# A bidirectional DeltaNet encoder on one core: two more pairs of buffers for the weights' parts, unnormalised keys, and three columns at the start of the output product

## The chip, the core and the metric

The kernel runs on one core of a Trainium2 chip. The metric is the device time of one execution in microseconds; lower is better. The kernel before was timed in three runs.

## The reference

A trunk of two layers works on 256 tokens of 2048 channels in float32. Layer 0 is a convolution module, layer 1 a bidirectional gated DeltaNet; a SwiGLU network with 5632 hidden channels stands behind each. RMS norms precede each part, and one stands at the end. The change lies in the DeltaNet:

```python
proj = h @ w_in                         # 2048 -> q | k | v | z | beta | a
qkv = silu(depthwise_conv_centred(qkv, w_conv))
q, k = l2norm(q), l2norm(k)             # 16 key heads of 128, each for 2 value heads
# each direction, chunks of 64, decays from a, weights beta:
kk = einsum("nbhcd,nbhed->nbhce", k, k)
lower = where(strict, kk * decay * beta, 0)
sol = triangular_solve(lower + eye, [v * beta, k * beta * exp(g)])
a_qk = where(tril, einsum(q, k) * decay, 0)     # q scaled by 128 ** -0.5
# a scan over chunks then gives the outputs o of either direction
o = o * rsqrt(mean(o * o) + eps) * norm_w * silu(z)
return o.reshape(S, 4096) @ w_out
```

## The kernel before, in words

Each weight matrix comes as tiles of 128 x 128. A matrix product (`products`, line 171) makes one column of 128 outputs for all 256 tokens. It loads raw weights in chunks of eight tiles (512 KB, three buffers "raw", `raw_weights`, 153), and splits four tiles at a time (a group) into a rounded high part and the rest as low part (`halves`, 160): ScalarE casts (line 167), VectorE subtracts (168). The two parts have four buffers each, "hi" and "lo" (`HI`); a caller that gives a pool of its own gets six (`XB`). Narrow products (the DeltaNet's) run three matmuls of 256 columns for each tile: high part on the activations' high part (197), high part on their low part (198), low part (199). Wide ones run one of 512 columns (193) and one of 256 (192).

`deltanet` (478) projects columns in the order written in `ORDER` (32): four columns of q and k for two key heads (`q`), four of v (`v`), single ones of the gate z (`z`), 96 in all, each of four groups. After each group `step` advances `now` and lets generators go on that are due; a `yield n` waits for n groups. They run beside the projections at a higher priority:

- `dn_norm` (655) sums the squares of q and k, turns the sums so that tokens lie on partitions, takes the power -1/2 into `rt` (672, 673), turns that back, stores it to DRAM, loads the keys' norms spread over all partitions (`rb`) and multiplies the keys (685). Then `dn_front` (698) makes the Gram products kk and kq (709), empties them (712), applies the decays (733 to 737) and stores the matrices `am`. `dn_fill` (741) copies blocks into the workspace S.
- After every second group of heads `dn_lanes` (750) inverts 32 x 32 blocks on VectorE in S, T, w0, w1, pd and F, and `dn_inverse` (819) joins them to larger blocks with matmuls.
- `dn_heads` (879) applies inverses and scans, normalises, turns, multiplies by the gate (`zr`, read back from DRAM, 946) and stores the result to `y_d` (948). `dn_turn` (954) turns the values v beforehand.

Behind the last column the remaining steps are run off, and the output product begins: each head's y is loaded (521), split (`ys`, 229 and 230) and used by all columns of `wout`. The first two columns (526) are made side by side, tile by tile, the others one after another.

The SBUF is full in the DeltaNet stage. Tiles named in `EARLY` lie in the pool `d0`, the others in `d1`; their tags, sizes and buffers stand in `DN` (534). The tiles ys lie where d0 was: the first `OUT0` in a pool `o0`, the rest in `o1`. The order of the instructions on each engine is made by a planner that simulates the program: where several could go, the one with the higher priority does. Loads and stores go through SyncE's queue in one order.

Of the kernel before, what the change touches and what calls it, by code (L numbers as in the profile page):

```python
# [7 lines left out]
F32 = mybir.dt.float32  # L8
F32R = mybir.dt.float32r
AF = mybir.ActivationFunctionType  # L10
ALU = mybir.AluOpType
# [16 lines left out]
HP = 550  # L28
OUT0 = 17
LAST = 2500  # L30
# [14 lines left out]
HI = 4  # L45
XB = 6


# [30 lines left out]
class Trunk:  # L79
    def __init__(self, ctx, tc, x, par, cst, pw1, pw2, win, wout, gu, dn, out):  # L80
# [13 lines left out]
        self.ahead = self.more = None  # L94
        self.turn = False
        self.cst = self.cp.tile([P, NCST], F32, name="cst_sb")
        self.par = self.cp.tile([P, NRES], F32, name="par_sb")
# [62 lines left out]
    def halves(self, raw, i, n, pool=None):  # L160

        nc = self.nc
        r = raw[:, i * P : (i + n) * P]
        hi, lo = ((pool or self.wp).tile([P, CS * P], F32R, tag=t, bufs=XB if pool else HI, name=self.nm(t))[:, : n * P]
                  for t in ("hi", "lo"))
# [312 lines left out]
    def deltanet(self, next_norm):  # L478
# [3 lines left out]
        self.c_d = dram.tile([NVH, 2 * S], F32, name="c_d")  # L482
        self.rn_d = [dram.tile([4, S], F32, name=f"rn_d{g}") for g in range(NKH // 2)]
        self.a_d = [dram.tile([P, 1024], F32, name=f"a_d{v}") for v in range(NVH)]
# [4 lines left out]
        with (tc.tile_pool(name="dn0", bufs=1, reuse_waits="tile") as d0,  # L489
              tc.tile_pool(name="dn1", bufs=1, reuse_waits="tile") as d1):  # L490
            self.d0, self.d1 = d0, d1
            self.dn_setup()
# [16 lines left out]
            while self.tasks:  # L509
                self.step()  # L510
            self.tasks = None

# [3 lines left out]
        with (tc.tile_pool(name="out0", bufs=1, reuse_waits="tile") as o0,  # L516
# [8 lines left out]
            self.norm_begin()  # L525
            first = self.products(self.wout[:2], NVH, ys, wide=True, tags=("lin", "lin"))
            for j in range(KD):
                for acc in first[j] if j < 2 else self.linear(self.wout[j], NVH, ys, wide=True):
                    nc.vector.tensor_tensor(self.h[j], acc, self.h[j], op=ALU.add)
                self.norm_tile(j, *next_norm)  # L530
# [3 lines left out]
    DN = {  # L534
        "t": (S, 2), "u": (S, 2), "th": (S, 2), "s2": (S, 3), "qk": (S, 4), "sq": (S, 2), "rb": (2 * S, 1), "kk": (4 * P, 1), "kq": (4 * P, 1),
        "cb": (2 * S, 2), "e": (768, 2), "am": (1024, 2), "ar": (1024, 2), "zr": (S, 1), "xd": (16 * P, 2),
        "w0": (1024, 1), "w1": (1024, 1), "pd": (1024, 2), "F": (256, 2), "pb": (16 * P, 2), "z32": (8 * P, 1), "z64": (8 * P, 1), "bl": (8 * 64, 1),
        "w1s": (S, 2), "w2s": (S, 2), "rx": (S, 2), "ot": (S, 4), "on": (S, 2), "v": (S, 6),
        "stk": (1024, 1), "tri": (1024, 1), "na": (1, 1), "nwh": (1, 1), "dg": (128, 1), "cr": (64, 1),
        "os": (8, 2), "rn": (P, 1), "rt": (8, 4), "rs": (S, 1),  # L540
    }

    EARLY = {"stk", "tri", "z32", "z64", "bl", "xd", "w0", "w1", "pd", "F", "cb", "e", "am", "kk", "kq", "rb", "qk", "rn", "rs", "sq"}

# [9 lines left out]
    def dn_setup(self):  # L554
        nc = self.nc
        self.S, self.T = self.d("stk"), self.d("tri")
        self.z32, self.z64, self.bl, self.pb = self.d("z32"), self.d("z64"), self.d("bl"), [self.d("pb"), self.d("pb")]
        for t in (self.z32, self.z64, self.bl, *self.pb):
            nc.gpsimd.memset(t, 0.0)
        nc.gpsimd.memset(self.S, 0.0)  # L560
        nc.gpsimd.memset(self.T, 0.0)
        nc.gpsimd.memset(fv(self.T, 0, (33, 32)), 1.0)
        self.na, self.nwh = self.d("na"), self.d("nwh")
        nc.scalar.activation(self.na, self.p("alog"), AF.Exp)
        nc.vector.tensor_scalar(self.na, self.na, -1.0, None, op0=ALU.mult)
        nc.vector.tensor_scalar(self.nwh, self.p("nw"), 0.5, None, op0=ALU.mult)

# [87 lines left out]
    def dn_norm(self, g, act, sqs, xd):  # L655
# [12 lines left out]
        for b in range(2):  # L668
            nc.tensor.transpose(tp[:, 4 * b : 4 * b + 4], rs[:, b * P : (b + 1) * P], self.mat("ident")[:4, :4])
        rt = self.d("rt")  # L670
        self.rt[g] = rt
        nc.vector.tensor_scalar(rt, tp[:, :8], 4e-6, None, op0=ALU.add)
        nc.gpsimd.tensor_tensor(rt, rt, self.c("mhalf").broadcast_to([P, 8]), op=ALU.pow)
        yield STEP
        nc.tensor.transpose(tp[:8, P:], rt, self.mat("ident"))
        rn = self.d("rn", 8)
        nc.scalar.copy(rn, tp[:8, P:])
        for b in range(2):
            nc.sync.dma_start(self.rn_d[g][:, b * P : (b + 1) * P], rn[4 * b : 4 * b + 4])
        rb = self.d("rb")  # L680
        keys = self.rn_d[g].rearrange("(h r) s -> r h s", r=2)[1]
        nc.sync.dma_start(rb.rearrange("p (r s) -> p r s", r=2), keys.partition_broadcast(P))
        for r in range(2):
            k = act[2 * r + 1]
            nc.vector.tensor_tensor(k, k, rb[:, r * S : (r + 1) * S], op=ALU.mult)
        yield LAG
        yield from self.dn_front(g, act, xd)
# [10 lines left out]
    def dn_front(self, g, qk, xds):  # L698
# [3 lines left out]
        for h in range(2):  # L702
            q, k = qk[2 * h], qk[2 * h + 1]
            grams = []
            for x, tag in ((k, "kk"), (q, "kq")):
# [5 lines left out]
                gs = self.d(tag)  # L711
                nc.scalar.activation(gs, ga, AF.Copy, scale=1.0 if x is k else P ** -0.5)
                grams.append(gs)
# [27 lines left out]
    def dn_fill(self, x, xd):  # L741

        for q in range(4):
            pr = slice(32 * q, 32 * q + 32)
# [5 lines left out]
    def dn_lanes(self, inv):  # L750
# [11 lines left out]

        L, tm = self.d("w0"), self.d("w1")
        V.transpose(nt(L), tr(S))
# [6 lines left out]
        at = lambda r, c: c * 32 + r  # L771
        R = self.d("w1")

# [15 lines left out]
        for s in (4, 8, 16):  # L789
# [25 lines left out]
        V.transpose(tr(tb), nt(tm))  # L815
        V.transpose(tr(tt), tr(tm))
        inv += [tt, tb]

# [60 lines left out]
    def dn_heads(self, g):  # L879
# [46 lines left out]

        osv, rq = fv(os, 0, (4, 2), (2, 2), (1, 2)), fv(rt, 0, (2, 2), (0, 2), (4, 2))
        nc.vector.tensor_tensor(osv, osv, rq, op=ALU.mult)
        nc.vector.tensor_tensor(osv, osv, rq, op=ALU.mult)
        nc.vector.tensor_scalar(os, os, 1.0 / P, self.c("eps6"), op0=ALU.mult, op1=ALU.add)  # L930
        nc.gpsimd.tensor_tensor(os, os, self.c("mhalf").broadcast_to([P, 8]), op=ALU.pow)
# [22 lines left out]
    def dn_turn(self, n, s2, at):  # L954
        nc = self.nc
        while self.now < at:
            yield 1
        tp = self.pst("g")
        for b in range(2):
            nc.tensor.transpose(tp[:, b * P : (b + 1) * P], s2[:, b * P : (b + 1) * P], self.mat("ident"))  # L960
        v = self.d("v")
        nc.scalar.activation(v, tp[:, :S], AF.Copy, scale=0.5)
        self.v[n] = v
# [109 lines left out]
```

## Time and profile before

| | us |
|---|---|
| median of three runs | 2854.71 (2853.86 to 2856.81) |
| the profiled execution | 2851.51 |
| its span in the trace | 2849.7 |
| TensorE busy with matmuls | 2772.4 |
| VectorE busy | 2074.2 |
| ScalarE busy | 1753.7 |
| DeltaNet stage, from and to | 1102 to 1921 |

The span goes from the first to the last instruction of the program. Matmuls are pipelined: one starts before the one ahead has ended, so a busy TensorE is not TensorE at its peak. Idle time is put down to what released the engine, and PEld is TensorE's weight load. A line such as L168 is a line of the kernel before.

### The profile page before, as it was taken

Reading aid. Unit: us, or ns where it says so; the run is one execution under the profiler, and the core shown is the slowest. Engines: PE = TensorE matmul, PEld = TensorE weight load, DVE = VectorE, ACT = ScalarE, POOL = GpSimd, SP = SyncE. Lnnn points to the kernel's source line nnn. Section 1 sums busy time; section 2 is a strip of 40 time slices with the busy share of each in tenths; the row PEclk is TensorE's granted clock in tenths of the full one; section 3 lists DMA queues with packets and bytes.
Section 4 is the critical chain, followed back from the end, with each engine's and each line's share of the span. In section 5 each row is a group of like instructions: output and inputs, shape, how many; then the busy total and the mean of one; then the engine's idle time right before and its main releaser. Section 6 shows DMA issues by size and latency. Waiting matters only on the chain.

```text
span 2849.7 us, 50209 instructions
## 1 busy us (share of the span) xinstructions
PE 2772.4 (97%) x18200; PEld 2523.5 (89%) x18200; DVE 2074.2 (73%) x3895; ACT 1753.7 (62%) x3654; POOL 367.1 (13%) x427
## 2 busy tenths in 40 slices
PE   8997999999999999999999999999999999999998
PEld 8997888888888889888999999998888888888887
DVE  7999876666666667789897989756666666665555
ACT  8877555555554445667778787765455555555443
POOL 3763310000000111000000000001110000000111
PEclk9998999999999999999999999999999999999999
DMA  5442565555566665765555655576565555556664
GB/s 185 141 143 98 196 208 191 189 189 191 187 188 195 200 198 173 230 216 176 194 191 184 214 193 198 165 247 205 190 209 190 188 189 191 188 190 185 191 190 137
DMA packets 174104, 536.05 MB, mean 188 GB/s; under 512 B 19264, under 2 KB 46208, under 8 KB 173856
## 3 DMA queue, kind: packets, MB, share of 16 engines
q1 hardware_dynamic: 172560, 531.55, 58.5%
q8 instruction: 142, 2.33, 0.3%
q10 hardware_dynamic: 1296, 1.30, 0.1%
q14 instruction: 106, 0.87, 0.1%
HBM read 503.31 MB, written 29.46 MB: 187 GB/s over the span
## 4 chain that ended last, share of the span: by engine, by line
PE 79%; DVE 8%; DMA 5%; ACT 4%; issue 2%; POOL 2%; SPq 0%; DVEq 0%; POOLq 0%; ACTq 0%
PE acc L193 39%; PE acc L192 20%; PE acc L199 5%; PE acc L197 5%; PE acc L198 5%; DVE lo L168 2%; POOL a L377 2%; PE psa L849 1%; PE psb L891 1%; ACT hi L167 1%; PE psb L914 1%; DVE r L385 1%; PE acc L195 1%; ACT m L376 1%; DMA y_d<-zr 1%
## 5 line engine op out<-in xcount | busy, mean ns | idle before, releaser
L168 DVE TENSOR_TENSOR lo<-raw,hi 128x512 fp32r<-128x512 f32 x1764 | 1257.2, 716 | 621.9 <-ACT hi L167 612.0
L167 ACT CAST hi<-raw 128x512 fp32r<-128x512 f32 x1764 | 1083.0, 619 | 851.4 <-PE acc L193 664.5
L193 PE MATMUL acc<-xs,hi 128*128 128x512 f32 x2816 | 967.3, 392 | 0.0
L192 PE MATMUL acc<-xs,lo 128*128 128x256 f32 x2640 | 744.1, 282 | 0.0
L197 PE MATMUL acc<-xs,hi 128*128 128x256 f32 x2064 | 590.1, 288 | 16.8 <-ACT hi L167 10.0
L193 PEld LDWEIGHTS acc<-xs,hi 128*128 128x128 f32 x2816 | 517.0, 188 | 99.4
L199 PE MATMUL acc<-xs,lo 128*128 128x256 f32 x2064 | 590.9, 289 | 14.2 <-DVE lo L168 13.7
L198 PE MATMUL acc<-xs,hi 128*128 128x256 f32 x2064 | 587.3, 286 | 0.4 <-DVE xs L246 0.3
L192 PEld LDWEIGHTS acc<-xs,lo 128*128 128x128 f32 x2640 | 498.4, 189 | 8.4
L193 PE MATMUL acc<-hs,hi 128*128 128x512 f32 x1408 | 486.8, 391 | 0.0
L199 PEld LDWEIGHTS acc<-xs,lo 128*128 128x128 f32 x2064 | 391.9, 191 | 27.5 <-DVE lo L168 21.4
L197 PEld LDWEIGHTS acc<-xs,hi 128*128 128x128 f32 x2064 | 394.0, 191 | 24.0 <-ACT hi L167 14.6
L198 PEld LDWEIGHTS acc<-xs,hi 128*128 128x128 f32 x2064 | 394.7, 191 | 4.9 <-issue 3.2
L192 PE MATMUL acc<-hs,lo 128*128 128x256 f32 x1376 | 388.3, 282 | 0.0
L193 PEld LDWEIGHTS acc<-hs,hi 128*128 128x128 f32 x1408 | 262.4, 188 | 53.0
L192 PEld LDWEIGHTS acc<-hs,lo 128*128 128x128 f32 x1376 | 260.0, 189 | 1.6
L458 POOL TENSOR_TENSOR tg<-tg,rstd 128x256 f32<-128x256 f32 x88 | 65.7, 747 | 905.5 <-ACT tg L457 905.5
L193 PE MATMUL acc<-ys,hi 128*128 128x512 f32 x512 | 178.3, 396 | 2.4 <-DVE ys L230 2.4
L377 POOL TENSOR_TENSOR a<-a,m 128x256 f32<-128x256 f32 x170 | 148.7, 875 | 98.1 <-ACT m L376 86.3
L192 PE MATMUL acc<-ys,lo 128*128 128x256 f32 x496 | 139.0, 285 | 1.9 <-DVE lo L168 1.9
L256 POOL TENSOR_TENSOR sq<-h 128x256 f32<-128x256 f32 x59 | 54.7, 928 | 555.4 <-DVE h L469 382.2
L633 DVE SCALAR_TENSOR_TENSOR u<-t,par_sb,u 128x254 f32<-128x254 f32 (+1 forms) x256 | 120.1, 478 | 1.3 <-ACT u L629 0.4
(231 smaller groups left out, 2890.6 us busy)
## 6 DMA issues: line engine op xcount, KB each, us to landing
raw<-in_gu SPq DMA_DIRECT2D x352, 512.0 KB, 4.4
raw<-in_win SPq DMA_DIRECT2D x194, 512.0 KB, 4.0
raw<-in_dn SPq DMA_DIRECT2D x160, 512.0 KB, 3.6
raw<-in_pw SPq DMA_DIRECT2D x94, 512.0 KB, 3.9
raw<-in_wout SPq DMA_DIRECT2D x64, 512.0 KB, 3.6
a_d<-am SPq DMA_DIRECT2D x32, 512.0 KB, 5.7
ar<-a_d SPq DMA_DIRECT2D x32, 512.0 KB, 3.3
raw<-in_dn SPq DMA_DIRECT2D x32, 256.0 KB, 3.6
```

The source lines that it names most:

```text
L167: nc.scalar.copy(hi, r)
L168: nc.vector.tensor_tensor(lo, r, hi.bitcast(F32), op=ALU.subtract)
L192: nc.tensor.matmul(acc[:, S:], lo, a[:, :S], start=False, stop=False)
L193: nc.tensor.matmul(acc, hi, a, start=first, stop=last)
L195: nc.tensor.matmul(acc[:, S:], lo, a[:, :S], start=False, stop=False)
L197: nc.tensor.matmul(acc[:, :S], hi, a[:, :S], start=first, stop=False)
L198: nc.tensor.matmul(acc[:, :S], hi, a[:, S:], start=False, stop=False)
L199: nc.tensor.matmul(acc[:, :S], lo, a[:, :S], start=False, stop=last)
L256: (nc.vector if last else nc.gpsimd).tensor_tensor(sq, h, h, op=ALU.mult)
L377: nc.gpsimd.tensor_tensor(acc, acc, m, op=ALU.add)
L458: nc.gpsimd.tensor_tensor(tg, tg, rstd, op=ALU.mult)
L633: nc.vector.scalar_tensor_tensor(u[:, lo:hi], t[:, lo + s : hi + s], w(i), u[:, lo:hi], op0=ALU.mult, op1=ALU.add)
```

## The change

Every third split in the DeltaNet stage takes its two tiles from d1, where each has two buffers: six in all. Room for these 8 KB a partition comes from d0: rb and rn are gone, w1 is replaced by the workspace S itself, and pd and F have one buffer in place of two. As S is now written until `dn_lanes` is done, `dn_fill` waits for that. The keys are not normalised any more: their factor is applied where the Gram products are emptied, in two instructions, each with a scale from `rt`, and on the other side at the emptying of the turned values, also in two. `rt` has 24 columns: the factors squared, the factors, and half of their reciprocals. The output product begins with three columns, and 26 tiles ys lie in o0.

```diff
-OUT0 = 17
+OUT0 = 26
+MORE = 2
@@ halves
+        self.nsplit += 1
+        bufs = XB if pool else HI
+        if self.parts is not None and self.nsplit % 3 == 0:
+            pool, bufs = self.parts, MORE
-        hi, lo = (... bufs=XB if pool else HI ...)
+        hi, lo = (... bufs=bufs ...)
@@ deltanet
-            self.d0, self.d1 = d0, d1
+            self.d0, self.d1, self.parts = d0, d1, d1
...
-            self.tasks = None
+            self.tasks = self.parts = None
-            first = self.products(self.wout[:2], NVH, ys, wide=True, tags=("lin", "lin"))
+            first = self.products(self.wout[:3], NVH, ys, wide=True, tags=("lin", "lin", "lin"))
             for j in range(KD):
-                for acc in first[j] if j < 2 else self.linear(...):
+                for acc in first[j] if j < 3 else self.linear(...):
@@ DN, EARLY
-  "rb": (2 * S, 1), "w1": (1024, 1), "pd": (1024, 2), "F": (256, 2), "rn": (P, 1), "rt": (8, 4),
+  "pd": (1024, 1), "F": (256, 1), "rt": (24, 4),
@@ dn_norm
+        nc.vector.tensor_scalar(rt[:, :8], tp[:, :8], 4e-6, None, op0=ALU.add)
+        nc.gpsimd.tensor_tensor(rt[:, 8:16], rt[:, :8], self.c("mhalf").broadcast_to([P, 8]), op=ALU.pow)
+        nc.vector.scalar_tensor_tensor(rt[:, 16:24], rt[:, :8], 0.5, rt[:, 8:16], op0=ALU.mult, op1=ALU.mult)
+        nc.vector.tensor_tensor(rt[:, :8], rt[:, 8:16], rt[:, 8:16], op=ALU.mult)
         self.rt[g] = rt
-        nc.vector.tensor_scalar(rt, tp[:, :8], 4e-6, None, op0=ALU.add)
-        nc.gpsimd.tensor_tensor(rt, rt, self.c("mhalf").broadcast_to([P, 8]), op=ALU.pow)
         yield STEP
-        nc.tensor.transpose(tp[:8, P:], rt, self.mat("ident"))
-        rn = self.d("rn", 8)
-        nc.scalar.copy(rn, tp[:8, P:])
-        for b in range(2):
-            nc.sync.dma_start(self.rn_d[g][:, b * P : (b + 1) * P], rn[4 * b : 4 * b + 4])
-        rb = self.d("rb")
-        ...
-        nc.sync.dma_start(rb.rearrange("p (r s) -> p r s", r=2), keys.partition_broadcast(P))
-        for r in range(2):
-            k = act[2 * r + 1]
-            nc.vector.tensor_tensor(k, k, rb[:, r * S : (r + 1) * S], op=ALU.mult)
-        yield LAG
@@ dn_front
-                nc.scalar.activation(gs, ga, AF.Copy, scale=1.0 if x is k else P ** -0.5)
+                for a in range(2):
+                    r = slice(2 * a * P, 2 * (a + 1) * P)
+                    nc.scalar.activation(gs[:, r], ga[:, r], AF.Copy, scale=self.rt[g][...])
@@ dn_fill
+        while self.filled:
+            yield 1
+        self.filled = x == 1
@@ dn_lanes
-        L, tm = self.d("w0"), self.d("w1")
+        L, tm = self.d("w0"), S
-        R = self.d("w1")
+        R = S
-        tm = self.d("w1")
+        tm = S
...
+        self.filled = False
@@ dn_turn
-        while self.now < at:
+        while self.now < at or n // 4 not in self.rt:
             yield 1
-        nc.scalar.activation(v, tp[:, :S], AF.Copy, scale=0.5)
+        for b in range(2):
+            c = slice(b * P, (b + 1) * P)
+            i = 16 + 4 * b + n % 4 // 2 * 2 + 1
+            nc.scalar.activation(v[:, c], tp[:, c], AF.Copy, scale=rt[:, i : i + 1])
```

The factors that the keys no longer carry are also taken into account in `dn_setup` and at the end of `dn_heads` (lines 566 and 927 to 930), by other constants and other columns of `rt`.

## Rows read from the trace of the kernel before

**Rows 1.** The head of the profile's page: the span, then the busy time of each engine with its share of the span and its number of instructions.

```profile
span 2849.7 us, 50209 instructions
...
PE 2772.4 (97%) x18200; PEld 2523.5 (89%) x18200; DVE 2074.2 (73%) x3895; ACT 1753.7 (62%) x3654; POOL 367.1 (13%) x427
```

**Rows 2.** Busy time by stretch (us from the span's start: length, then busy time and number of instructions of TensorE's matmuls, its weight loads, VectorE, ScalarE and GpSimd, then granted clock, DMA share, GB/s). The first row is the DeltaNet stage, the second its end and the beginning of the output product, the third the rest of the output product.

```profile
1102.00:1921.00 819.00, 786.63 (x6437) 754.44 (x6437) 684.32 (x1489) 596.84 (x1453) 32.10 (x21) 0.99 0.61 200
1921.00:1945.00 24.00, 19.71 (x93) 16.22 (x93) 13.75 (x31) 10.77 (x25) 0.00 (x0) 0.86 0.64 206
1944.00:2101.00 157.00, 157.00 (x906) 138.93 (x905) 107.72 (x162) 78.11 (x130) 24.95 (x30) 1.00 0.61 195
```

**Rows 3.** Waits of TensorE's matmuls from 1098 to 1935 us: who waited for whom, us in total, times, the longest.

```profile
PE acc L199 <- DVE lo L168: 11.5, 17, 1.8
PE acc L197 <- DVE t L628: 3.8, 3, 1.8
PE acc L197 <- ACT hi L167: 3.3, 4, 1.4
PE acc L193 <- DVE ys L230: 2.4, 1, 2.4
PE psg L709 <- DVE qk L685: 2.4, 3, 1.0
...
PE acc L192 <- DVE lo L168: 1.9, 1, 1.9
...
PE psb L891 <- ACT hi L167: 0.9, 1, 0.9
```

**Rows 4.** TensorE's timeline at the beginning of the DeltaNet stage, undisturbed: the first and the last of 17 matmuls, each of 256 columns (start, duration, line, operation).

```profile
1100.07 0.28 PE L198 MATMUL acc<-xs,hi 128*128 128x256 f32 x1
...
1101.93 0.28 PE L199 MATMUL acc<-xs,lo 128*128 128x256 f32 x1
```

**Rows 5.** The same view at 1185.7 us, behind a wait of 1.69 us for the low part of a weight tile.

```profile
1185.74 0.39 PE L199 MATMUL acc<-xs,lo 128*128 128x256 f32 x1 [1.69 <-DVE lo L168]
1185.96 0.37 PE L197 MATMUL acc<-xs,hi 128*128 128x256 f32 x1
```

**Rows 6.** ScalarE's timeline ahead of that wait.

```profile
1182.05 3.16 ACT L747 ACTIVATE stk<-xd 32x256 f32<-32x256 f32 x8 [0.63 <-DVE xd L735]
1185.23 0.62 ACT L167 CAST hi<-raw 128x512 fp32r<-128x512 f32 x1
```

**Rows 7.** Waits of VectorE in the DeltaNet stage (1098 to 1935 us).

```profile
DVE zr L947 <- DMA zr<-z_d: 19.2, 13, 2.6
DVE qk L685 <- DMA rb<-rn_d: 12.6, 5, 3.9
...
DVE am L733 <- DMA a_d<-am: 9.7, 4, 3.4
```

**Rows 8.** Waits of ScalarE in the same stretch.

```profile
ACT hi L167 <- PE acc L198: 68.3, 109, 2.0
...
ACT hi L167 <- DMA raw<-in_win: 17.7, 12, 2.9
```

**Rows 9.** Two links of the chain of waits that ended last (start, length): the norms' way through DRAM, for group 6.

```profile
1701.35 2.94 DMA rn_d<-rn
1704.30 3.75 DMA rb<-rn_d
```

**Rows 10.** Groups of instructions on ScalarE from 1098 to 1935 us (line, operation, shapes, count | busy us, mean ns of one | idle before, and what ended it).

```profile
L167 ACT CAST hi<-raw 128x512 fp32r<-128x512 f32 x397 | 240.0, 616 | 109.9 <-PE acc L198 68.3 <-DMA raw<-in_win 17.7 <-DMA raw<-in_wout 6.7
...
L935 ACT ACTIVATE ot<-ot,os 128x128 f32<-128x128 f32 x64 | 19.6, 396 | 0.0
...
L944 ACT ACTIVATE on<-psb,nwh 128x256 f32<-128x256 f32 x32 | 14.5, 469 | 2.6 <-DVE zr L947 1.8 <-PE psb L942 0.7
...
L962 ACT ACTIVATE v<-psg 128x256 f32<-128x256 f32 x32 | 12.0, 376 | 2.6 <-PE psg L960 2.6
...
L712 ACT ACTIVATE kq<-psg 128x512 f32<-128x512 f32 x16 | 9.4, 590 | 5.3 <-PE psg L709 5.3
```

**Rows 11.** The same on VectorE.

```profile
L168 DVE TENSOR_TENSOR lo<-raw,hi 128x512 fp32r<-128x512 f32 x397 | 268.6, 685 | 38.9 <-ACT hi L167 34.8 <-issue 1.7
...
L685 DVE TENSOR_TENSOR qk<-qk,rb 128x256 f32<-128x256 f32 x16 | 6.1, 421 | 12.6 <-DMA rb<-rn_d 12.6
```

**Rows 12.** Two stretches of 40 us whose granted clock is below full (columns as in rows 2).

```profile
1178.00:1218.00 40.00, 38.12 (x298) 36.19 (x297) 28.74 (x58) 28.93 (x67) 1.64 (x1) 0.96 0.77 246
...
1738.00:1778.00 40.00, 39.48 (x329) 39.49 (x330) 38.17 (x103) 25.93 (x67) 0.00 (x0) 0.96 0.61 202
```

**Rows 13.** The end of the stage in stretches of 10 us (columns as in rows 2).

```profile
1920.00:1930.00 10.00, 6.61 (x35) 5.08 (x33) 4.15 (x7) 3.93 (x9) 0.00 (x0) 1.00 0.51 158
1930.00:1940.00 10.00, 9.11 (x36) 7.82 (x37) 5.96 (x15) 4.32 (x11) 0.00 (x0) 0.66 0.67 224
...
1950.00:1960.00 10.00, 10.00 (x59) 8.86 (x58) 7.60 (x12) 5.07 (x9) 1.73 (x2) 1.00 0.70 225
```

**Rows 14.** The loads of the heads' outputs from DRAM: their count, durations and first and last start.

```profile
L521 SPq DMA_DIRECT2D y<-y_d x32: 319/382/1582, 1864.0 to 1939.9; - x32
```

**Rows 15.** The stretch of 10 us with the highest DMA rate (last column, GB/s).

```profile
1870.00:1880.00 10.00, 9.15 (x80) 8.89 (x79) 7.84 (x18) 7.84 (x22) 0.00 (x0) 1.00 0.94 306
```

**Rows 16.** The DMA issues of the output product's weights (count, size, median us from issue to landing).

```profile
raw<-in_wout SPq DMA_DIRECT2D x64, 512.0 KB, 3.6
```

More of the change, by code (lines that the diff above doesn't have):

```diff
@@ L95, in __init__ @@
         self.turn = False
+        self.parts, self.nsplit = None, 0
         self.cst = self.cp.tile([P, NCST], F32, name="cst_sb")
@@ L163, in halves @@
         r = raw[:, i * P : (i + n) * P]
-        hi, lo = ((pool or self.wp).tile([P, CS * P], F32R, tag=t, bufs=XB if pool else HI, name=self.nm(t))[:, : n * P]
-                  for t in ("hi", "lo"))
+        self.nsplit += 1
+        bufs = XB if pool else HI
+        if self.parts is not None and self.nsplit % 3 == 0:
+            pool, bufs = self.parts, MORE
+        hi, lo = ((pool or self.wp).tile([P, CS * P], F32R, tag=t, bufs=bufs, name=self.nm(t))[:, : n * P] for t in ("hi", "lo"))
         with self.tc.high_priority(WP):
@@ L482, in deltanet @@
         self.c_d = dram.tile([NVH, 2 * S], F32, name="c_d")
-        self.rn_d = [dram.tile([4, S], F32, name=f"rn_d{g}") for g in range(NKH // 2)]
         self.a_d = [dram.tile([P, 1024], F32, name=f"a_d{v}") for v in range(NVH)]
@@ L525, in deltanet @@
             self.norm_begin()
-            first = self.products(self.wout[:2], NVH, ys, wide=True, tags=("lin", "lin"))
+            first = self.products(self.wout[:3], NVH, ys, wide=True, tags=("lin", "lin", "lin"))
             for j in range(KD):
-                for acc in first[j] if j < 2 else self.linear(self.wout[j], NVH, ys, wide=True):
+                for acc in first[j] if j < 3 else self.linear(self.wout[j], NVH, ys, wide=True):
                     nc.vector.tensor_tensor(self.h[j], acc, self.h[j], op=ALU.add)
@@ L534 @@
     DN = {
-        "t": (S, 2), "u": (S, 2), "th": (S, 2), "s2": (S, 3), "qk": (S, 4), "sq": (S, 2), "rb": (2 * S, 1), "kk": (4 * P, 1), "kq": (4 * P, 1),
+        "t": (S, 2), "u": (S, 2), "th": (S, 2), "s2": (S, 3), "qk": (S, 4), "sq": (S, 2), "kk": (4 * P, 1), "kq": (4 * P, 1),
         "cb": (2 * S, 2), "e": (768, 2), "am": (1024, 2), "ar": (1024, 2), "zr": (S, 1), "xd": (16 * P, 2),
-        "w0": (1024, 1), "w1": (1024, 1), "pd": (1024, 2), "F": (256, 2), "pb": (16 * P, 2), "z32": (8 * P, 1), "z64": (8 * P, 1), "bl": (8 * 64, 1),
+        "w0": (1024, 1), "pd": (1024, 1), "F": (256, 1), "pb": (16 * P, 2), "z32": (8 * P, 1), "z64": (8 * P, 1), "bl": (8 * 64, 1),
         "w1s": (S, 2), "w2s": (S, 2), "rx": (S, 2), "ot": (S, 4), "on": (S, 2), "v": (S, 6),
         "stk": (1024, 1), "tri": (1024, 1), "na": (1, 1), "nwh": (1, 1), "dg": (128, 1), "cr": (64, 1),
-        "os": (8, 2), "rn": (P, 1), "rt": (8, 4), "rs": (S, 1),
+        "os": (8, 2), "rt": (24, 4), "rs": (S, 1),
     }
-    EARLY = {"stk", "tri", "z32", "z64", "bl", "xd", "w0", "w1", "pd", "F", "cb", "e", "am", "kk", "kq", "rb", "qk", "rn", "rs", "sq"}
+    EARLY = {"stk", "tri", "z32", "z64", "bl", "xd", "w0", "pd", "F", "cb", "e", "am", "kk", "kq", "qk", "rs", "sq"}
     def d(self, tag, rows=P):
@@ L565, in dn_setup @@
         nc.vector.tensor_scalar(self.na, self.na, -1.0, None, op0=ALU.mult)
-        nc.vector.tensor_scalar(self.nwh, self.p("nw"), 0.5, None, op0=ALU.mult)
+        nc.vector.tensor_scalar(self.nwh, self.p("nw"), 0.5 * P ** -0.5, None, op0=ALU.mult)
     def dn_gates(self):
@@ L711, in dn_front @@
                 gs = self.d(tag)
-                nc.scalar.activation(gs, ga, AF.Copy, scale=1.0 if x is k else P ** -0.5)
+                for a in range(2):
+                    r = slice(2 * a * P, 2 * (a + 1) * P)
+                    nc.scalar.activation(gs[:, r], ga[:, r], AF.Copy, scale=self.rt[g][:, 4 * a + 2 * h + 1 : 4 * a + 2 * h + 2])
                 grams.append(gs)
@@ L816, in dn_lanes @@
         V.transpose(tr(tt), tr(tm))
+        self.filled = False
         inv += [tt, tb]
@@ L925, in dn_heads @@
         self.heads_done[g] = True
-        osv, rq = fv(os, 0, (4, 2), (2, 2), (1, 2)), fv(rt, 0, (2, 2), (0, 2), (4, 2))
+        osv, rq = fv(os, 0, (4, 2), (2, 2), (1, 2)), fv(rt, 8, (2, 2), (0, 2), (4, 2))
         nc.vector.tensor_tensor(osv, osv, rq, op=ALU.mult)
         nc.vector.tensor_tensor(osv, osv, rq, op=ALU.mult)
-        nc.vector.tensor_scalar(os, os, 1.0 / P, self.c("eps6"), op0=ALU.mult, op1=ALU.add)
+        nc.vector.tensor_scalar(os, os, P ** -2.0, self.c("eps6"), op0=ALU.mult, op1=ALU.add)
         nc.gpsimd.tensor_tensor(os, os, self.c("mhalf").broadcast_to([P, 8]), op=ALU.pow)
@@ L960, in dn_turn @@
             nc.tensor.transpose(tp[:, b * P : (b + 1) * P], s2[:, b * P : (b + 1) * P], self.mat("ident"))
-        v = self.d("v")
-        nc.scalar.activation(v, tp[:, :S], AF.Copy, scale=0.5)
+        v, rt = self.d("v"), self.rt[n // 4]
+        for b in range(2):
+            c = slice(b * P, (b + 1) * P)
+            i = 16 + 4 * b + n % 4 // 2 * 2 + 1
+            nc.scalar.activation(v[:, c], tp[:, c], AF.Copy, scale=rt[:, i : i + 1])
         self.v[n] = v
```

1 line of the change is left out of this document (removed).

## The prediction

> **What bounds the kernel now.** TensorE does: on the page it is busy for 97% of the span, VectorE for 73%, ScalarE for 62% [rows 1]. I read the page first, then busy time by stretch, since the change lies in the DeltaNet stage and in the product behind it. From 1102 to 1921 us matmuls are busy for 786.6 of 819 us, at a granted clock of 0.99, so 32.4 us are idle; the 24 us behind them have a clock of 0.86, and from 1944 us on the output product has no idle time at all [rows 2]. Everything that can be won is thus between 1100 and 1945 us. The waits of TensorE's matmuls there tell what it lacks [rows 3]: mostly the low part of a weight tile from VectorE (11.5 us in 17 waits), the high part from ScalarE (3.3 and 0.9 us), an accumulator that VectorE empties late (3.8 us), the normalised keys (2.4 us). The timeline shows one of these waits [rows 5], and ScalarE ahead of it [rows 6]: it copies blocks for 3.16 us between two casts. Undisturbed, matmuls start (1101.93 - 1100.07) / 16 = 0.116 us apart [rows 4], so a group of four weight tiles (12 matmuls) is 1.4 us of work. With four buffers, three groups lie ready: 4.2 us. An engine that is away for longer, counting the way back through ScalarE and then VectorE, leaves TensorE dry. VectorE is away often: it waits in its queue for transfers, 12.6 us for the norms' way through DRAM, 19.2 us for gates, 9.7 us for a store that still reads its buffer [rows 7]. And buffers are what the split waits for: ScalarE's casts stood 68.3 us, in 109 waits, until matmuls gave a buffer back, and 17.7 us for raw weights [rows 8].
>
> **The change part by part.** The sum is made against the profiled execution, 2851.51 us (a span of 2849.7 us and 1.8 us around it), 3.2 us below the median of 2854.71 us; I take the difference off the median. About 0.2% (5.7 us) is what a measurement of this kernel can tell from no change.
>
> *Six buffers.* Every third split of the stage goes to two further pairs of buffers. They are used in turn, so five groups can lie ready, 5 x 1.4 = 7.0 us, 2.8 us more than before. The longest wait that they are to cover is 1.8 us [rows 3]. The waits for parts sum to 15.7 us in 22 waits. A matmul lasts 0.28 us and the next starts 0.12 us behind it, so a wait loses some 0.17 us more than its idle time shows: 22 x 0.17 = 3.7 us. Together 19.4 us. All would go if each wait stood alone; several follow one another before the buffers have filled again, and where raw weights are late more buffers of parts are empty too. Between none and 19.4 us I take three quarters: -14.5 us. What is late next are the accumulators (3.8 us) and the heads' own links, which stay.
>
> *Clock.* Behind the wait at 1185.7 us matmuls start 0.22 us apart instead of 0.116 [rows 5]: the lower of the clock's two levels. The stretch of 40 us there has a clock of 0.96, and so has that from 1738 us [rows 12]: 4% of 40 us, 1.6 us each. In the whole stage 1% of 819 us, 8 us, is lost in this way [rows 2]. I count the two: -3.2 us, between 0 and -8.
>
> *Keys without norm.* Eight times the change removes a transpose, a copy, two stores, a load that spreads the norms over all partitions, and two VectorE multiplies of 0.42 us (16, 6.1 us [rows 11]) that stood 12.6 us in front of VectorE's queue [rows 7]. The matmuls of dn_front waited 2.4 us for them in three waits, 2.9 us with the hidden part: -2.9 us. The VectorE time frees low parts, and is counted above. On SP's queue 24 transfers go, and the raw weights behind them move up.
>
> *Scales at the evictions.* In place of the multiply, each Gram product (32) is emptied by two instructions of 256 columns with a scale from a tile, and each of 32 value tiles by two of 128 columns. The nearest rows [rows 10]: one of 512 columns took 590 ns, one of 256 with such a scale 469 ns, so 2 x 469 - 590 = 348 ns more, 11.1 us in all. A value tile took 376 ns, two halves at 396 ns would take 416 ns more, 13.3 us in all. ScalarE, busy for 597 of 819 us [rows 2], has room, and casts go ahead of it by priority; the one buffer "g" in PSUM is held some 0.35 us longer, 64 times. On the path between -1 us (half an eviction done sooner) and 22 us (each held in full); the next user of "g" comes two steps later, some 4 us, so I take +2 us. The added VectorE operations on 8 columns cost nothing: they are done three steps, 6 us, ahead of their use, on an engine busy for 684 of 819 us [rows 2].
>
> *One workspace in dn_lanes.* S serves as w1, and pd and F have one buffer each. All three are written and read by VectorE in one order, so nothing is awaited that wasn't. The new wait is dn_fill's: it holds until the lanes of the pair before are done. Counted in steps (one per group, 384 in the stage, so 819 / 384 = 2.1 us each): the lanes of groups 0 and 1 run from step 68 to 100, the fill of group 2 comes at 112; for group 4 it is 180 against 188, for group 6 it is 256 against 264. It never binds, and behind it stands only its own generator. dn_turn's wait for rt doesn't bind either, as the norms of a group are done tens of steps before its values.
>
> *The end.* dn_norm loses a LAG of six steps, so the last pair's lanes, inverse and heads come up to 6 x 2.1 = 13 us earlier, and the DRAM way of 2.94 + 3.75 us [rows 9] goes with it. That meets the stall at the end: where 59 matmuls run in 10 us, 35 and 36 ran from 1920 to 1940 us, at a clock of 0.66 in the second half [rows 13]: 47 too few, 47 x 10 / 59 = 8.0 us. The last heads' outputs are read back by 1939.9 us [rows 14]. Three columns instead of two give 32 x 0.347 = 11 us more work at that point (0.347 us a tile and column: 157 us / 906 x 2 [rows 2]). But here parts is None: four buffers again, three raw tiles, and three columns take three of each at once. I bound the opener's own price below (12.4 us). Between -8 and +4 us I take -3.
>
> *Removed from TensorE.* Eight transposes, 8 x 0.116 = 0.9 us. The move of tiles from o1 to o0 changes no time: the loads begin once the inverse is done, before as after.
>
> Sum: -14.5 - 3.2 - 2.9 + 2 - 3 - 1 = -22.6 us; 2854.7 - 22.6 = **2832 us**. The order on each engine comes from a planner's simulation, which I can't foresee; that is the widest part of the range.
>
> **The rivals.** *A: the cover only moves the wait* (chance 0.20). In-order VectorE still stands before zr and am for 28.9 us [rows 7], and raw weights, still in three buffers, come late as before [rows 8]; the parts go half as well, -10 us, the clock gives nothing, and the end nothing: with the keys -2.9 and the evictions +2, some -10 us: 2844 us. For it speaks that ScalarE's 17.7 us are at the raw tiles already; against it that 68.3 us are at the parts.
>
> *B: the opener starves* (0.08, the slower side). Three columns need three raw tiles of 512 KB at once, 1.57 MB, 5.1 us at the highest rate seen, 306 GB/s [rows 15] (one alone lands in 3.6 us [rows 16]), then a cast of 0.62 and a subtraction of 0.69 us [rows 10, 11]: 6.4 us, against 12 x 0.347 = 4.2 us that the group in work covers; 2.2 us at each of three changes of chunk, 6.7 us. At each of seven changes of group two of three columns are split only when TensorE gives their buffers back, some 0.8 us late, 5.7 us. Sum 12.4 us, and with the clock at half in it up to 20. This decides if the body gives less than the opener takes: with A's -10 and 20, 2865 us. Against it: TensorE stands still there today anyway.
>
> *C: more was lost than idle time shows* (0.12). Then every term of the sum pays in full: 19.4 + 8 + 2.9 + 8 + 1 = 39 us, 2815 us. Idle time of pipelined matmuls understates, as the 0.17 us above show. The Trainium skill (Perfetto Trace Analysis, Identifying the Most-Contended Engine) says that matmul busy time is a poor measure and the weight loads' share a better one. By it 819 - 754.4 = 64.6 us of the stage are open [rows 2], twice the 32.4; the trace agrees in direction, but small products and transposes are in that too.
>
> *D: nothing that can be measured* (0.05), if the planner spends the room on running further ahead at the wrong places.
>
> **How the numbers follow.** The forecast has 0.55, and its own range is 2822 to 2842 us (parts at 8 to 19 us, the end from -8 to +4). The range of 8 in 10 takes in A and part of C: 2818 to 2850. Faster by over 0.2%, below 2849: forecast 0.54, C 0.12, A 0.15, 0.81 in all. Slower, above 2860.4: B and a stray 0.01, 0.08. The rest, 0.11, is within.
>
> **What would show it.** Right: the waits of matmuls for low and high parts fall under 6 us between 1100 us and the stage's end; no wait for rb; ScalarE busy some 20 us longer; the first ys matmul some 10 us earlier, and no slice of 10 us with under 50 matmuls at the end. Wrong: as many waits for parts, now behind raw tiles (A); idle time or half clock in the first 35 us of the output product (B); matmuls that wait for kk, kq or v (the evictions were under-priced).

## The result and the profile after

The changed kernel takes **2830.63 us** (median of four runs, 2829.84 to 2833.88) against 2854.28 us for the kernel before: a ratio of **0.9923 [0.9911, 0.9936]**. That is 23.6 us less by the medians and 22 us by the ratio, which the comparisons below use. The profiled execution took 2831.13 us. The head of its page, to be read against [rows 1]:

```profile
span 2829.3 us, 50192 instructions
...
PE 2754.5 (97%) x18192; PEld 2508.4 (89%) x18192; DVE 2070.5 (73%) x3895; ACT 1760.6 (62%) x3710; POOL 367.6 (13%) x427
```

The span is 20.4 us shorter. Nearly all of it (20.1 us) lies between the stage's beginning at 1102 us and the end of the output product, at 2099.8 us before and 2079.7 us after. By stretch, columns as in [rows 2]; the first row now ends where the first matmul of the output product stands (1878.6 us, before 1913.3 us):

```profile
1102.00:1879.00 777.00, 755.67 (x6333) 729.89 (x6332) 671.24 (x1468) 590.91 (x1472) 30.71 (x20) 1.00 0.62 204
1879.00:1945.00 66.00, 53.81 (x301) 45.73 (x301) 35.38 (x71) 33.35 (x81) 5.78 (x6) 0.90 0.58 186
1944.00:2079.00 135.00, 135.00 (x779) 119.40 (x778) 90.77 (x133) 66.62 (x110) 20.73 (x24) 1.00 0.60 191
```

The first row shows a body at a granted clock of 1.00, where before there were five drops to the lower level, 17.1 us together. The second row is the other side: the output product opens 35 us earlier, but the 66 us behind its opening hold 12.2 us without work at a clock of 0.90, where the 32 us behind the opening held 4.3 us before. TensorE's waits in the body, as in [rows 3]:

```profile
PE pssum L668 <- ACT sq L656: 3.9, 3, 2.4
PE acc L202 <- DVE t L633: 3.0, 2, 1.6
...
PE acc L202 <- ACT hi L172: 2.0, 3, 1.2
PE acc L204 <- DVE lo L173: 1.8, 5, 0.9
```

The low parts, first in [rows 3] with 11.5 us in 17 waits, stand at 1.8 us in 5, and high and low parts together at 3.8 us in 8, up to the opening (2.5 us more for low parts behind it). No wait for normalised keys is left, and none names kk, kq or v. What ScalarE's casts wait for, as in [rows 8]:

```profile
ACT hi L172 <- PE acc L203: 49.2, 65, 2.6
ACT hi L172 <- DMA raw<-in_win: 43.0, 27, 4.8
```

The wait for a free buffer of parts fell by 19 us, and that for raw weights rose by 25 us: the raw tiles are what is late next. The two evictions that changed, as in [rows 10]:

```profile
L968 ACT ACTIVATE v<-psg,rt 128x128 f32<-128x128 f32 x64 | 20.1, 364 | 6.6 <-DVE rx L908 4.3 <-PE psg L963 1.9
...
L710 ACT ACTIVATE kk<-psg,rt 128x256 f32<-128x256 f32 x32 | 13.4, 469 | 2.4 <-PE psg L705 2.2
```

They cost 469 and 364 ns each, as the nearest rows had said (469 and 396), but kk, kq and v together keep ScalarE busy 16 us longer than before, and no wait of TensorE names them. The end in stretches of 10 us, as in [rows 13], and the two longest waits of TensorE between 1879 and 1945 us:

```profile
1900.00:1910.00 10.00, 9.05 (x55) 7.81 (x54) 4.71 (x9) 6.97 (x17) 1.91 (x1) 1.00 0.45 134
1910.00:1920.00 10.00, 6.59 (x37) 5.13 (x35) 3.01 (x5) 3.76 (x8) 0.00 (x0) 0.94 0.66 230
1920.00:1930.00 10.00, 3.64 (x11) 3.06 (x12) 2.62 (x7) 1.16 (x4) 0.00 (x0) 0.50 0.28 91
1930.00:1940.00 10.00, 10.00 (x53) 8.70 (x53) 9.29 (x17) 6.41 (x13) 3.87 (x5) 0.88 0.53 173
```

```profile
PE acc L198 <- DVE ys L235: 8.6, 1, 8.6
PE acc L197 <- DVE lo L173: 2.5, 4, 1.1
```

From 1920 to 1930 us only 11 matmuls run, at the lower clock: all three columns stand for 8.6 us before one head's output. Why it is late shows in SyncE's queue at the end of the stage (start, duration, operation):

```profile
1908.15 0.38 SPq L951 DMA_DIRECT2D y_d<-zr  x1
...
1913.22 0.33 SPq L949 DMA_DIRECT2D zr<-z_d  x1
...
1915.79 0.32 SPq L951 DMA_DIRECT2D y_d<-zr  x1
...
1917.96 0.32 SPq L949 DMA_DIRECT2D zr<-z_d  x1
...
1921.73 0.32 SPq L951 DMA_DIRECT2D y_d<-zr  x1
1923.41 0.32 SPq L949 DMA_DIRECT2D zr<-z_d  x1
1926.00 0.32 SPq L951 DMA_DIRECT2D y_d<-zr  x1
```

There is one buffer zr. So the last heads go one behind the other: a store to DRAM, a load of the next gate into the buffer that the store has freed, a multiply, the next store. The last store starts at 1926.0 us, 4.5 us earlier than before (1930.5 us), although TensorE was ready 35 us earlier.

### The profile page after: what moved, and what is told of

It is laid out like the page before. It is cut to its first block, busy times and chain, and to the rows that moved or that the text cites. A ratio compares the mean times of both kernels' runs of the same rounds, so it can differ in the third digit from the quotient of the medians.

```text
span 2829.3 us, 50192 instructions
## 1 busy us (share of the span) xinstructions
PE 2754.5 (97%) x18192; PEld 2508.4 (89%) x18192; DVE 2070.5 (73%) x3895; ACT 1760.6 (62%) x3710; POOL 367.6 (13%) x427
## 4 chain that ended last, share of the span: by engine, by line
PE 81%; DVE 6%; ACT 5%; DMA 5%; issue 2%; POOL 1%; SPq 0%; DVEq 0%; POOLq 0%; ACTq 0%
PE acc L198 40%; PE acc L197 20%; PE acc L204 5%; PE acc L203 5%; PE acc L202 5%; DVE lo L173 2%; POOL a L382 1%; DMA raw<-in_win 1%; ACT hi L172 1%; PE psa L852 1%; PE psb L894 1%; DMA y_d<-zr 1%; PE acc L200 1%; PE psb L917 1%; DVE r L390 1%
```

## The experiments

Ratios are to the kernel before, run beside each. The last five columns are in us, from the profiled executions. "Opening" is the first matmul of the output product; idle time of TensorE and time at the lower clock are given for the body (1102 us to the opening) and the end (from there to the last matmul of the output product; behind 1945 us only three_alone, four_buffers, six_three and four_columns have any of it); "last store" is the start of the last store of a head's output. Two profiled executions lie over 5 us above the median of their kernel: short_chain's (2840.28 against 2834.9 us) and four_columns' (2849.22 against 2843.45 us).

| kernel | ratio | opening | idle, body / end | lower clock, body / end | last store |
|---|---|---|---|---|---|
| before | 1 | 1913.3 | 32.4 / 4.3 | 17.1 / 6.8 | 1930.5 |
| the change | 0.9923 | 1878.6 | 21.3 / 12.2 | 0 / 13.7 | 1926.0 |
| six_alone | 0.9977 | 1871.9 | 17.1 / 22.5 | 10.2 / 30.7 | 1924.5 |
| keys_alone | 0.9956 | 1896.0 | 23.8 / 9.2 | 17.1 / 10.2 | 1918.5 |
| three_alone | 1.0027 | 1916.5 | 33.9 / 8.9 | 20.5 / 3.4 | 1934.8 |
| two_columns | 0.9955 | 1880.9 | 17.0 / 18.6 | 20.5 / 17.1 | 1925.9 |
| four_buffers | 0.9979 | 1901.8 | 26.9 / 7.8 | 17.1 / 0 | 1931.2 |
| six_three | 0.9982 | 1875.7 | 20.2 / 23.7 | 6.8 / 27.3 | 1931.9 |
| keys_lag | 0.996 | 1893.0 | 23.1 / 13.3 | 10.2 / 13.7 | 1919.9 |
| short_chain | 0.9948 | 1886.8 | 20.1 / 13.1 | 17.1 / 10.2 | 1934.8 |
| zr_four | 0.9913 | 1870.9 | 16.1 / 12.8 | 10.2 / 6.8 | 1919.7 |
| opener_parts | 0.9911 | 1866.2 | 14.0 / 10.4 | 6.8 / 13.7 | 1913.9 |
| all_three | 0.9921 | 1864.8 | 14.3 / 13.2 | 6.8 / 10.2 | 1913.1 |
| four_columns | 0.997 | 1915.9 | 37.8 / 0.2 | 49.4 / 5.2 | 1909.5 |

**One part at a time.** *six_alone*: the kernel before, with the fifth and sixth buffer and the shared workspaces that make room for them.

```diff
+ if self.parts is not None and self.nsplit % 3 == 0: pool, bufs = self.parts, MORE
- L, tm = self.d("w0"), self.d("w1")
+ L, tm = self.d("w0"), S
```

> The kernel before with the shared workspaces and six buffers alone: keys still normalised through DRAM, two columns at the start of the output product. My theory: waits for parts fall from 15.7 to under 6 us, the clock's drops mostly go, and the time is 12 to 20 us under the kernel before, 2834 to 2842 us; the drop of VectorE's wait for rb adds at most 4 us to that in the full change. Rival (VectorE's queue is what mattered): with rb still awaited for some 12 us the waits for parts stay over 10 us and the gain is under 6 us.

Measured 2847.61 us, 0.9977 [0.9967, 0.9986], 6.6 us less. Its two stretches:

```profile
1102.00:1872.00 770.00, 752.88 (x6299) 729.49 (x6299) 668.51 (x1452) 570.84 (x1387) 31.12 (x20) 0.99 0.63 204
1872.00:1945.00 73.00, 50.51 (x264) 42.42 (x263) 34.28 (x75) 36.83 (x97) 4.40 (x4) 0.79 0.58 180
```

Idle time in the body falls from 32.4 to 17.1 us, and the opening comes 41 us earlier. But the heads end only 6 us earlier (1924.5 us), so 22.5 of the 73 us behind the opening are idle, at a clock of 0.79. The buffers do in the body what they are for; alone, most of it is given back at the end.

*keys_alone*: the changed kernel with four buffers, two columns and the workspaces and the 17 tiles ys in o0 of before, so the unnormalised keys by themselves.

```diff
- self.d0, self.d1, self.parts = d0, d1, d1
+ self.d0, self.d1, self.parts = d0, d1, None
```

> The kernel before with unnormalised keys alone: four buffers, the old workspaces, two columns. My prediction put 2.9 us on the matmuls' wait for the normalised keys and took 2 us off for the evictions; by it 2850 to 2856 us. If the shorter way from the keys to the lanes brings the heads' end forward by the 13 us that the prediction counted, 2840 to 2847 us.

Measured 2840.4 us, 0.9956 [0.9941, 0.9971], 12.6 us less: the only one of the three that pays much alone.

```profile
1102.00:1896.00 794.00, 770.15 (x6370) 743.81 (x6369) 677.84 (x1479) 599.93 (x1493) 29.80 (x19) 0.99 0.62 202
1896.00:1945.00 49.00, 39.78 (x221) 34.31 (x220) 30.31 (x57) 25.58 (x56) 4.13 (x5) 0.90 0.61 192
```

```profile
L948 SPq DMA_DIRECT2D y_d<-zr x4: 319/322/327, 1901.4 to 1918.5; - x4
```

The body is 8.6 us less idle, and the last heads' outputs (the row gives the first and last start of the last four stores) are stored 12 us earlier than before.

*three_alone*: the kernel before, whose output product begins with three columns.

```diff
- first = self.products(self.wout[:2], NVH, ys, wide=True, tags=("lin", "lin"))
+ first = self.products(self.wout[:3], NVH, ys, wide=True, tags=("lin", "lin", "lin"))
```

> The kernel before with three columns at the start of the output product, nothing else. Theory now: the heads' chain ends near 1926 us in every version, the projections end when TensorE lets them, and the columns at the start are filler between the two. Before has 32 us between its first product of ys (1913 us) and the end of its trouble (1945 us), with 8 us lost in it; a third column covers most of that: 2844 to 2850 us. Rival: without more buffers three columns starve, and the time is 2854 us or more.

Measured 2860.44 us, 1.0027 [1.0016, 1.0039], **7.7 us more**. The wait that rival B had priced is there, from 1916 to 1960 us:

```profile
PE acc L192 <- DVE lo L168: 6.5, 8, 3.4
```

Three columns take parts faster than four buffers give them, 6.5 us in 8 waits, while TensorE had waited for heads for 2.4 us only in this place [rows 3]: there is little to fill, and something to lose.

**One part undone.** *two_columns* is the change with `self.wout[:2]`; *four_buffers* is the change with `self.parts = None` in the stage.

> The changed kernel with two columns at the start of the output product instead of three. Its trace shows a wait of 8.6 us there for the last heads' outputs. If the third column is filler that covers this wait (32 tiles, 11 us of work), two columns make the wait longer by up to 10 us: 2834 to 2842 us. Rival, the starving opener of the prediction: three columns are split too late, and two win 2 to 6 us: 2825 to 2829 us. If the planner merely puts other projections there, 2829 to 2833 us.

> The changed kernel without the two further pairs of buffers; its keys, workspaces and three columns stay. My theory: the buffers carry the gain of the stage's body. Waits of matmuls for the parts come back to 10 to 16 us between 1100 us and the opener (3.8 us with six), two to five drops to half clock come back, and the time rises from 2830.6 to 2842 to 2850 us. Rival: the gain comes from the norms' way through DRAM that is gone, and from the room that this gives VectorE; then the waits for parts stay under 8 us and the time is 2831 to 2836 us.

two_columns: 2840.17 us, 0.9955 [0.994, 0.997]; the waits for the heads' outputs at the end are two, 8.3 and 7.2 us, and the third column fills about one of them. four_buffers: 2846.83 us, 0.9979 [0.9969, 0.9988]; waits for parts in the body are back, though with 8.6 us they stay under the 10 to 16 us expected. The largest wait is another: for `pd`, the inverted blocks that VectorE makes in dn_lanes.

```profile
PE psa L852 <- DVE pd L818: 8.5, 4, 3.2
PE acc L204 <- DVE lo L173: 6.2, 13, 1.0
...
PE acc L202 <- ACT hi L172: 2.4, 4, 1.4
```

*six_three* (six_alone with three columns) completes the set.

> Six buffers and shared workspaces with three columns, keys still normalised through DRAM. Six buffers alone gave 2847.6 us: the projections end 42 us earlier, and 22 us of the 73 behind them were idle. Theory: the third column (11 us of filler) turns that into time, 2834 to 2841 us, and the keys' part is the rest to 2830.6. Rival: the unnormalised keys are what lets the chain end in time, and without them the third column wins under 3 us: 2845 to 2850 us.

Measured 2848.93 us, 0.9982 [0.9972, 0.9991]. From 1876 to 1945 us:

```profile
1876.00:1945.00 69.00, 46.17 (x244) 38.57 (x242) 27.61 (x63) 32.53 (x91) 1.63 (x1) 0.80 0.55 180
```

Without the new keys the heads end at 1931.9 us, and the third column, used up at the same late output, does not help: 22.8 us are idle here, 23.7 with what follows.

The eight settings together, as ratio x 2854 us: keys are worth -12.6 us alone, -6.2 with six buffers, -13.7 with three columns, -16.9 with both; six buffers -6.6, -0.3 with keys, -12.8 with three columns, -16.0 with both; three columns +7.7, +1.5 with six buffers, +6.6 with keys, -9.2 with both. (The workspaces go with six buffers, and in four_buffers too, where they are a rival: of the +6.6 us of the third column beside the keys, some or all can be theirs. Against keys_alone, four_buffers is no more idle at the end, 7.8 against 9.2 us, but 3.1 us more in the body, and its matmuls wait 8.5 us for `pd`, against 0.8 us. No run has the keys with the workspaces, four buffers and two columns, or the workspaces alone.) With intervals of some 3 to 4 us either way on each ratio, the differences of 10 us and more between settings stand: alone the three add to -11.5 us, together they give -22.

**The lag.** *keys_lag* is keys_alone with `yield LAG` put back ahead of `yield from self.dn_front(...)`; *short_chain* is the change with the other lag cut, `yield LAG` to `yield 1` behind dn_lanes.

> Keys alone, with the LAG of six steps put back in dn_norm that the change removes. Keys alone gave 2840.4 us, 12.8 under the kernel before, and its last heads' output came 12 us earlier (1918.5 against 1930.5 us). If the six steps carry that, the last output comes at 1926 us or later and the time goes back to 2847 to 2852 us. If VectorE's queue, free of the wait for rb, carries it, the time stays at 2838 to 2843 us.

> The changed kernel with a lag of one step instead of six between dn_lanes and dn_inverse. In its trace 15 us lie there for the last pair. Theory: the heads' chain sets the end, so the last output comes 8 to 10 us earlier than 1926 us, the wait of 8.6 us for it goes under 3 us, and the time is 2820 to 2825 us. Rival: the planner's order at the end sets it, and the time stays within 2828 to 2834 us.

keys_lag: 2840.01 us, 0.996 [0.9946, 0.9974], the same as keys_alone.

```profile
L949 SPq DMA_DIRECT2D y_d<-zr x4: 320/323/326, 1902.7 to 1919.9; - x4
```

The last store moves by 1.4 us, not by the 13 us that six steps of 2.1 us would be. short_chain: 2834.9 us, 0.9948 [0.9933, 0.9963], 4 us slower than the change by the medians and 7 by the ratios, whose intervals just touch; the last store is at 1934.8 us. The 15 us that I had expected between the last pair's lanes and its inverse are not there: in the change its first matmul waits for the lanes and starts as they end.

```profile
1788.79 2.00 PE L852 MATMUL psa<-pd,z 128*128 128x64 f32 x16 [0.59 <-DVE pd L818]
```

Work ordered by priority runs ahead of the step in which it is written, so neither of these two lags in steps was time. Whether the short lag is really slower, and why, is not settled: its waits in the body are those of the change, and the 17.1 us at the lower clock, some 8.5 us of work, belong to the profiled execution, the slowest of its four (see the last section).

**The end.** *zr_four* is the change with four buffers zr.

```diff
- "zr": (S, 1)
+ "zr": (S, 4)
```

> The changed kernel with four buffers instead of one for zr, in which a head's gate is read back, multiplied and stored. With one buffer each of the last four heads goes through store, load, multiply in turn, some 5 to 6 us each, from 1908 to 1926 us. If that row of waits sets the arrival of the last outputs, the last store comes 8 to 12 us earlier, TensorE's wait of 8.6 us and the half clock around it mostly go, and the time is 2818 to 2824 us. Rival: the heads' own chain or SyncE's queue sets it, and the time stays within 2828 to 2832 us.

Measured 2828.71 us, 0.9913 [0.9898, 0.9928]: the turn through one buffer is gone, the last store comes 6.3 us earlier, and the single wait of 8.6 us is no longer there. Only 1.9 us of it show in the time, and the intervals overlap: 12.8 us at the end are still idle, in many small waits, and the body has 10.2 us at the lower clock. The single buffer is thus a cause of that one wait; most of the time lost at the end stays without it.

*opener_parts* is zr_four with two more buffers of parts for the output product's opening, too (and 22 tiles ys in o0); *all_three* is opener_parts with the short lag.

```diff
+ self.parts, self.nsplit = o0, 0
  first = self.products(self.wout[:3], NVH, ys, wide=True, tags=("lin", "lin", "lin"))
+ self.parts = None
```

> Four zr buffers as in zr_four (2828.7 us), and two further pairs of parts for the third of the three columns at the start of the output product, so that each column has two pairs. In zr_four TensorE waits 3.7 us there for low parts and 0.9 us for high ones. If that is the price of opening with three columns on four pairs, these waits go and the time is 2822 to 2826 us. If the raw tiles, still three, are what comes late, 2827 to 2831 us.

> The short lag, four zr buffers and the opener's own parts together. If the three add, 2812 to 2820 us; if the short chain already covers the end, 2819 to 2824 us; if the planner's order undoes one by another, 2826 us or more.

opener_parts: 2824.91 us, 0.9911 [0.9896, 0.9926], the lowest median of all, but not to be told from the change. all_three: 2828.42 us, 0.9921 [0.9906, 0.9936]. The stretches of opener_parts and its last stores:

```profile
1102.00:1866.00 764.00, 750.04 (x6298) 727.74 (x6296) 665.65 (x1454) 582.97 (x1444) 29.74 (x21) 1.00 0.63 204
1866.00:1945.00 79.00, 68.61 (x384) 58.63 (x383) 46.69 (x96) 44.26 (x115) 7.79 (x8) 0.91 0.65 209
```

```profile
L953 SPq DMA_DIRECT2D y_d<-zr x4: 319/342/383, 1912.3 to 1913.9; - x4
```

The body is the best of all (14.0 us idle), the last output is stored 12 us earlier than in the change, and still 10.4 us are idle at the end, because the opening has moved up by 12 us too.

*four_columns* is zr_four with four columns, whose parts lie in the room that the stage leaves (`pool=o1`).

> The changed kernel with four zr buffers and four columns at the start of the output product, with six buffers of parts and three more raw tiles of their own for them. Theory: between the last projection (about 1871 us) and the last ys (1930 us) TensorE has 59 us to fill with the heads' matmuls and 32 x 0.347 = 11 us for each column; the fourth, and parts that are split in time, take most of the 13 us that stand idle there with three: 2817 to 2824 us. Rival: the longest wait is for the heads' own matmuls, and filler changes nothing more: 2826 to 2830 us.

Measured 2843.45 us, 0.997 [0.9958, 0.9983].

```profile
1102.00:1916.00 814.00, 776.18 (x6390) 750.60 (x6388) 680.69 (x1497) 604.43 (x1514) 31.35 (x21) 0.97 0.62 201
1916.00:1945.00 29.00, 29.00 (x154) 25.32 (x155) 15.75 (x26) 13.47 (x25) 0.00 (x0) 0.91 0.57 185
```

```profile
PE acc L198 <- ACT hi L172: 7.4, 1, 7.4
PE psb L947 <- ACT ot L940: 5.8, 1, 5.8
```

```profile
1910.96 1.33 SPq L159 DMA_DIRECT2D raw<-in_wout  x3
1915.25 1.14 ACT L172 CAST hi<-raw 128x512 fp32r<-128x512 f32 x2 [2.20 <-DMA raw<-in_wout]
```

The end up to 1945 us has no idle time (29.00 of 29.00 us), but the opening had to wait until 1916 us. The 7.4 us are a wait for a high part, whose cast waited in turn for raw weights: SyncE issues their loads only at 1910.96 us, behind the last heads' stores. Whether the queue held them back or room that the stage still filled, no run separates. The body ran 49 us at the lower clock in this execution, the slowest of six.

## Why the prediction held, and where it did not

The sum was -22.6 us; -23.6 us were measured by the medians, -22 by the ratio. The trace of the change shows the mechanism that was forecast, fewer waits for parts. That the sum came so close is luck in part: a term that was too small, one with the wrong sign and one that was not seen made up for each other. Of the signs that were to show it right, the waits for parts and the missing wait for rb came; the opening was not some 10 but 35 us earlier, the end has slices with 37 and 11 matmuls, and idle time and the lower clock behind the opening, a sign of B, are there.

- **Six buffers, -14.5 us: the waits as forecast, the price only in company.** 15.7 us of waits for parts [rows 3] became 3.8 us. Undone in the change (four_buffers), the buffers are worth 16.0 us; of the waits behind that, 4.8 us are for parts (8.6 against 3.8) and 6.4 us for `pd` (8.5 against 2.1), which the sum did not have. Alone the buffers are worth 6.6 us, beside the keys with two columns 0.3 us, which the working, term by term, did not allow for.
- **Clock, -3.2 us: open.** In the two profiles all five drops in the body went, 17.1 us at half, some 8.5 us: the bound of 8, not the two drops that I counted. But their going is not shown to be the change's doing. two_columns, with the same buffers and less idle time in the body, has 20.5 us at the lower clock. And over the whole span the profiled execution of the kernel before has a mean granted clock of 0.990, where 42 others of the same kernel have 0.990 to 0.994, 0.992 in the mean; the four of the change have 0.991 to 0.992. The term should have been a range from the start.
- **Keys, -2.9 us: mis-sized.** Alone they are worth 12.6 us, [8.3, 16.8]. I had priced the matmuls that waited for keys, and put the rest into a step that the runs refute: the six steps of LAG (keys_lag). What else pays is not separated: VectorE's queue stands 12.6 us less for the norms [rows 7], 24 transfers leave SyncE's queue, and the way through DRAM leaves each chain of heads. No run divides these three. The last group's norms are taken 12 us earlier in keys_alone (the power at 1684.2 against 1696.2 us), so this chain is already 12 us ahead where that group's own way through DRAM would begin.
- **Evictions, +2 us: not seen.** The prices held (469 and 364 ns); no matmul of the trace after waits for kk, kq or v. ScalarE is busy 6.9 us longer on the page, where 20 were forecast; but the page counts time in which two instructions overlap once, and with each instruction counted in full it is 19.8 us (1922.0 against 1902.3 us).
- **The end, -3 us: wrong sign.** From the opening to 1945 us, idle time rose from 4.3 to 12.2 us and time at the lower clock from 6.8 to 13.7 us. The step that failed is the one that brought the last pair 13 us earlier: the last pair's lanes did end 9.7 us earlier (1788.7 against 1798.4 us), but the last store came only 4.5 us earlier, behind the single buffer zr, while the faster body brought the opening 35 us earlier. The third column was then needed to fill a gap that the change itself had opened (two_columns).
- **Workspaces, 0 us: not shown.** The matmuls that wait for `pd` are the inverse's first: 2.1 us in two waits in the body of the change, 1.3 us in two before, but 8.5 us in four in four_buffers, and none in six_alone, both with the same workspaces. These never ran by themselves, so whether they or something else makes the lanes late there stays open.

**The rivals.** *A* named the right thing (raw tiles late: 17.7 to 43.0 us on ScalarE), but it did not reach TensorE, whose waits for high parts are 2.0 us in the body. *B* is true of the third column alone (three_alone, +7.7 us against 12.4 forecast); in the change the opener's waits for low parts are 2.5 us, as the columns stand before a late output anyway. *C* held in its idea: from 1102 us to the output product's end 20.1 us went, of which TensorE's idle time is only some 3 us. To see the rest, I took for each pair of successive matmuls the time from start to start, less the lower quartile of the same pair of shapes over the fourteen kernels' traces (the end reaches to the output product's last matmul):

| us lost | before | the change | keys_alone | six_alone | three_alone |
|---|---|---|---|---|---|
| body | 85.5 | 57.8 | 69.4 | 52.9 | 87.4 |
| end | 9.0 | 18.9 | 12.7 | 34.9 | 15.3 |

In the body of the change, waits over 0.3 us fell from 39.1 to 24.7 us, the lower clock from 7.9 to 0, the losses below 0.3 us each, which no view of idle time shows, from 38.5 to 33.1. So the body gained 27.7 us, 7.9 of them by the clock alone, and the end took 9.9 us back; six_alone gained 32.6 and gave back 25.9. The Trainium skill (Perfetto Trace Analysis, Identifying the Most-Contended Engine) says that the weight loads' share tells more than that of the matmuls. The trace agrees in direction again: time without weight loads fell from 90.1 to 82.9 us between the same two points (997.8 us with 907.7 us of loads, 977.7 with 894.8). That is twice what idle time shows, and still only 7.2 of 20.1 us.

## What to carry to other kernels

Before you price more buffers in the middle of a stage, follow the chain that ends the stage: if it does not get shorter, TensorE arrives earlier and waits there instead, and the gain must be carried by work that can fill that place (here a third column, which cost time as long as there was no gap). Price a part within the setting in which it will run: alone the three parts gave 11.5 us, together 22. In an order made by priorities, a lag written in steps need not be time, as two here were not: look in the trace whether the engine waits there at all. And before you price a clock from one profile, look at the granted clock of the kernel's other executions.

## What the runs showed that was not expected

The same wait can be followed by a drop of the clock or not. At 1678 us, in the change and in short_chain, the same matmul waited 0.94 and 0.95 us (timelines of TensorE: start, duration, operation, idle time before it):

```profile
1678.41 0.39 PE L204 MATMUL acc<-xs,lo 128*128 128x256 f32 x1 [0.94 <-DVE lo L173]
```

```profile
1678.23 0.39 PE L204 MATMUL acc<-xs,lo 128*128 128x256 f32 x1 [0.95 <-DVE lo L173]
```

and the 20 us around it, from 1670 to 1690 us, in the same order (columns as in [rows 2]):

```profile
1670.00:1690.00 20.00, 17.93 (x150) 17.20 (x149) 12.41 (x30) 18.36 (x44) 2.01 (x1) 1.00 0.50 164
```

```profile
1670.00:1690.00 20.00, 18.64 (x116) 17.91 (x115) 10.98 (x26) 16.69 (x40) 2.01 (x1) 0.74 0.47 152
```

The first ran at 1.00 throughout. The second had 10.24 us at the lower of the two levels, a mean of 0.74, and 34 fewer matmuls. What decides between them no run here shows, so the clock's part of any of these differences, up to half of the time at the lower level, is partly outside what the change does: in the thirteen kernels beside the one before, that time in the body was between 0 and 49.4 us. One kernel alone differs from execution to execution: 42 of the kernel before have a mean granted clock of 0.990 to 0.994 over their span. Between these two lie 0.4% of 2850 us, 11 us, which is 23 us at the lower level.
